# Attention of two layers rewritten: values as stationary column halves, probabilities weighed before their transpose

## The chip, the cores and the metric

The program runs on one core of one Trainium2 chip. The metric is device microseconds (us) of one execution; lower is better. The engines in the text are PE (matrix products and transposes), ACT (ScalarE), DVE (VectorE), POOL (GpSimd) and SP, which issues most DMAs.

## The reference

A two-layer transformer block for 256 tokens of width 1024, and one more attention layer behind it, all in float32. The layers, by the names that the kernel gives them:

- AB: `u = rms_norm(h)`; one wide projection `u @ w_in`; mixer A, 8 heads of 64: keys and values out of a latent of 256 (`w_uk`, `w_uv`), each query sees only the 64 keys that an index score ranks highest; mixer B, 8 heads of 64: causal softmax with a forget bias `cum[q] - cum[k]`; `h + concat(o_a, o_b) @ w_out`.
- MLP: `h + square(relu(rms_norm(h) @ w1)) @ w2`, hidden width 4096.
- C: 16 heads of 64 in two groups that share keys and values. Each head has three branches, each a softmax of its own, summed under sigmoid gates: `out = g0*o_c + g1*o_s + g2*o_w`, where o_c attends to 15 compressed blocks, o_s to selected blocks and o_w to a window. At 256 tokens o_s and o_w are two causal softmaxes over different keys and values. Then `h + o @ w_out`.
- MLP again, then the final norm.
- D: differential attention, 16 heads with two maps each, and its output projection.

For each query block of 128 tokens: `p = exp(s - m) / sum`, `o = p @ v`.

## The kernel before

The residual `h` stays in SBUF as two tiles of 128 tokens. Each weight block is loaded (SP), rounded to a high part `wH` (ACT or DVE) and a remainder `wL` (DVE), and each product is the sum of three PE products (H*H, H*L, L*H) in fp32r. Below, a *product* is one such instruction of 512 columns.

A softmax **map** is one head (in C one head and branch) on 256 queries. Its causal part is 128 x 128 for the first query block and 128 x 256 for the second, so a tile `E` of 128 x 384 holds it, queries on the partitions. The steps, for A, B and C alike:

1. `scores` or, in C, the fp32r products of `two_maps`: PE writes the scores into PSUM banks. In A, B and D two heads of 64 rows each run beside each other in the two row halves of the PE array.
2. `softmax_num`: DVE adds the mask and takes the minimum (two instructions), ACT takes the exponential with its sum (two instructions, each with a read of the accumulator).
3. `pv_part`: PE transposes E (three blocks) into a bank, ACT copies it into a tile `PT` (two of them), PE multiplies the transposed map (stationary, 128 columns) with the values (moving, 64 columns) in three products. In C `two_maps` does both branches of one head.
4. `finish`, once for four heads of A or B, or two of C: reciprocal of the sums, gates in C, DVE scales the output (queries on the partitions), in C two additions, then PE transposes it (`o_strand`), and it is rounded to H and L as the operand of the output projection. In C the compressed branch is multiplied for a whole group at once into a slot `oc` (`cmp_att`) and added here.

The division is thus made on the output. 48 maps go this way: 8 of A, 8 of B, 32 of C. D has maps of its own and keeps them.

**What sets the order.** All instructions are issued by a planner, `_Weaver`, at build time. Each piece of work is a strand, a Python generator that yields operations; the planner emits the operation that can start earliest by its own costs (`_Engine.cost`, `T`), ties by priority, so each engine's instruction stream is fixed when the program is built. An operation that more than one engine could do is yielded as a list, and the planner takes the smallest sum of ready time, cost and a toll (`W.toll`: 1.8 us for DVE in AB and C, 0.3 in D, 1.5 for POOL, none for ACT). Buffers are tokens: 8 PSUM banks, 8 `E`, 2 `PT`, 4 score tokens `S`, 14 slots of 4 KB per partition.

**The order of AB**: projections for the index, the small parts and A's queries, then `uk`, `uv`; A's attention; B's projections; B's attention; output rows 0 to 7. `out_proj` walks 4 rows of the weight over four pieces of the output, then for each piece the last 4 rows (in C: 7 rows, then the last).

Of the kernel before, what the change touches and what calls it, by code (L numbers as in the profile page):

```python
# [18 lines left out]
P = 128  # L19
# [82 lines left out]
class _Engine:  # L102
# [13 lines left out]
    def cost(self, name, a, kw):  # L116
# [16 lines left out]
        if kw.get("op") == ALU.pow:  # L133
            return 1e-3 * (300 + 165 * n)
# [127 lines left out]
def tile_kernel(ctx: ExitStack, tc: tile.TileContext, I: dict, out: bass.AP):  # L262
# [6 lines left out]
    slots = ctx.enter_context(tc.tile_pool(name="slots", bufs=14))  # L269
# [4 lines left out]
    NE, NPT, NS = 8, 2, 4  # L274
    W = _Weaver(B=8, E=NE, PT=NPT, S=NS, slot=14, n2=6, raw=3, w=8, rope=2, dup=3)
# [12 lines left out]
    HALF = 0  # L288
    T1W = 0
# [35 lines left out]
    def T(calls, beside=1):  # L325
        late = calls if callable(calls) else lambda: calls
        cost = work = 0.0
        for c in late():
            if len(c) == 3:
                cost += 0.109  # L330
                work += 0.053
            else:
                work += _free(c[0]) * (4 if c[1].dtype == F32 else 1) * c[1].shape[0] / 128 * 0.4167e-3
                cost += 0.003 + (4 * max(_free(c[0]), 128) if c[1].dtype == F32 else max(_free(c[0]), 256 if c[1].dtype == F32R else 128)) * 0.4167e-3
# [8 lines left out]
        return _Op("T", cost / beside, emit, None, work)  # L343
# [336 lines left out]
    def scores2(bs, qs, ks, stop=True):  # L680
        two = [scores(b, q, k, stop) for b, q, k in zip(bs, qs, ks)]
        return T([x for both in zip(*two) for x in both], 2)
# [12 lines left out]
    class Group:  # L695
# [7 lines left out]
        def start(self):  # L703
            if self.sums is None:
                self.sums = small(8, "sums", 6)

# [29 lines left out]

    def maps_strand(grp, qs, ks, evs, masks_of, vs, i, prio, bias=None):
        for e in evs:
            yield ("ev", e)
        yield ("acq", "E", 2)  # L740
        Es = [e384("E", NE) for _ in range(2)]
        masks = yield from masks_of(Es)
        yield ("acq", "S", 2)
        yield ("acq", "B", 2)
        bs = [bank(), bank()]
        yield scores2(bs, qs, ks, bias is None)
        if bias:
            yield T(bias(bs))
        grp.start()

        def free(te):
            W.give("B", te)
            W.give("S", te)

        def one(n):
            E = Es[n]
            yield from softmax_num(E, bs[n][:, 0:P], bs[n][:, P:3 * P], masks[n], grp.sums, 2 * (i + n), free)
            yield from pv_part(grp, E, vs[n], ((i + n) * P, (i + n) * P + 64), ((i + n) * P + 64, (i + n + 1) * P))

        W.spawn(one(1), prio + 1, W.end + 0.2)  # L760
        yield from one(0)
# [144 lines left out]
    def plan_ab():  # L906
        wv = kview(I["ab_w_in"][0])
        return dict(
            aqi=chunk(wv, [(784, 1296)], kpt=1), small=chunk(wv, [(512, 784), (1296, 1368), (2904, 2912)]),
            aq=chunk(wv, [(0, 512)]),  # L910
            uk=chunk(I["a_w_uk"][0].rearrange("(k p) h e -> p k (h e)", p=P), [(0, 384)], 2),
            uv=chunk(I["a_w_uv"][0].rearrange("(k p) h e -> p k (h e)", p=P), [(0, 512)], 2),
            bq=chunk(wv, [(1368, 1880)]), bk=chunk(wv, [(1880, 2392)]), bv=chunk(wv, [(2392, 2904)]),
            out=rows(kview(I["ab_w_out"][0]), range(8)))
# [12 lines left out]
    def layer_ab(pl, hin, hout):  # L927
# [144 lines left out]
        yield ("acq", "slot")  # L1072
        qA, qAev = kslot(slot()), pair()
        yield from proj(pl["aq"], heads_T(qA, qAev, -0.125), uop, uev)

        def ck(k, t):
            return ckH[:, k, t * P:(t + 1) * P], ckL[:, k, t * P:(t + 1) * P]

        yield ("acq", "slot", 2)
        kA, kAev = kslot(slot()), pair()  # L1080
        vA, vAev = slot().rearrange("p (t n) -> p t n", t=2), pair()
# [21 lines left out]

        yield from proj(pl["uk"], ev_k, ck, ckev)
        yield from proj(pl["uv"], ev_v(vA, rck, rckev, vAev), ck, ckev)
# [34 lines left out]
        def attention(qT, kT, v, evs, masks_of, bias, side, prio):  # L1140
            for g in range(2):
                def finish(grp, g=g):
                    rs = small(8, "rs", 4)
                    yield dve.reciprocal(out=rs, in_=grp.sums)
                    yield ("acq", "n2")
                    on = n2()
                    te = yield dve.tensor_tensor(
                        out=on.rearrange("p (t h d) -> p h t d", t=2, h=4),
                        in0=grp.ob.rearrange("p (h t d) -> p h t d", h=4, t=2),
                        in1=rs.rearrange("p (h t) -> p h t", h=4).unsqueeze(3).to_broadcast([P, 4, 2, 64]),  # L1150
                        op=ALU.mult)
                    W.give("B", te)
                    yield from o_strand(lambda j, t: on[:, t * S + j * P:t * S + (j + 1) * P],
                                        oH[side][:, 2 * g:2 * g + 2, :], oL[side][:, 2 * g:2 * g + 2, :],
                                        oev[4 * side + 2 * g:4 * side + 2 * g + 2])

                grp = Group(4, finish)
                for j in (0, 2):
                    hd = 4 * g + j
                    hi = [slice(0, 64), slice(64, 128)]  # L1160
                    vv = [[v[:, t, (hd + n) * 64:(hd + n + 1) * 64] for t in range(2)] for n in range(2)]
                    W.spawn(maps_strand(grp, [qT[x, hd // 2, :] for x in hi], [kT[x, hd // 2, :] for x in hi], evs,
                                        lambda Es, hd=hd: masks_of(hd, Es), vv, j, prio + hd,
                                        None if bias is None else (lambda bs, hd=hd: bias(bs, hd))), prio + hd)

        def masks_a(hd, Es):
            return [maskA, maskA]
            yield

        attention(qA, kA, vA, qAev + kAev + vAev + [maskev], masks_a, None, 0, 10)  # L1170
# [9 lines left out]
        def masks_b(hd, Es):  # L1180
            for n in range(2):
# [5 lines left out]
        def bias_b(bs, hd):  # L1187
            return [mm(bs[n][:, 0:3 * P], sel[:, hd + n, :], cumk, False, True) for n in range(2)]

        attention(qB, kB, vB, qBev + kBev + vBev + [cumev], masks_b, bias_b, 1, 20)  # L1190

        def opnd(k, t):
            return oH[k // 4][:, k % 4, t * P:(t + 1) * P], oL[k // 4][:, k % 4, t * P:(t + 1) * P]

        yield from out_proj(pl["out"], opnd, lambda k: oev[k], residual(hout))
# [8 lines left out]
    def layer_c(pl, hin, hout):  # L1204
# [185 lines left out]
        def cmp_att(g, Q, qev, oc, ocev):  # L1390
# [23 lines left out]
            summed = W.end  # L1414
            rc = small(16, "crc", 2)
            rcev = _Event()

            def sums():
# [4 lines left out]
                te = yield dve.tensor_tensor(out=rc.rearrange("p (t h) -> p t h", t=2),  # L1423
                                             in0=sc.rearrange("p (t h) -> p t h", t=2),
                                             in1=gates[:, :, 8 * g:8 * g + 8, 0], op=ALU.mult)
                rcev.set(te)

            W.spawn(sums(), 8 + 20 * g, summed)
            yield ("acq", "B")
            b = bank()  # L1430
            te = yield T([tr(b[:, t * P:(t + 1) * P], ec[:, t * P:(t + 1) * P]) for t in range(2)])
            yield ("acq", "n2")
# [422 lines left out]
```

## Time and profile before

| | |
|---|---|
| median of three runs | 924.11 us (922.16 to 925.39) |
| profiled execution | 921.53 us, span 919.4 us |
| PE busy in the span | 901.2 us, 98% |
| DVE, ACT, POOL busy | 64%, 56%, 12% |
| mean granted PE clock | 0.998 of full speed |

Start and end of the layers can be seen in PE's operands: AB ends with the first product of the MLP at 143.5 us, C reaches from about 325 to 464 us, D from 646 us to the end. A duration in the trace is that of one instruction from start to end; instructions of one engine overlap by some tenths of a us, so what one costs its engine is the distance from its start to the start of the next, called its pitch below. A timeline row with xN joins N like instructions.

### The profile page before, as it was taken

To read this page: it belongs to the slowest core of one execution; us is meant where nothing else is said; L and a number is where in the kernel's file an instruction comes from. 1 tells how busy PE (TensorE), PEld (TensorE's weight loads), DVE (VectorE), ACT (ScalarE), POOL (GpSimd) and SP (SyncE) were. 2 spreads that over 40 slices of the span, in tenths; PEclk is the share of its full clock that TensorE was granted. 3 is DMA by queue.
4 is the path that set the end of the run, shared out by engine and by line. 5 is a ranking of instruction groups with operands and counts; after the bars stand their busy time and mean duration, and the time that the engine had idled before them with its cause. 6 is when DMAs were issued, how large, how long until landed. Compare 5 with 4: busy or idle time off the path is not lost.

```text
span 919.4 us, 14126 instructions
## 1 busy us (share of the span) xinstructions
PE 901.2 (98%) x5196; PEld 766.9 (83%) x5196; DVE 586.6 (64%) x1230; ACT 518.2 (56%) x1025; POOL 106.4 (12%) x149
## 2 busy tenths in 40 slices
PE   8999999999999999999999999999999999999998
PEld 6778888999999878888789999998877778777786
DVE  5688646544454457766654445444878878697781
ACT  5666858455544564787575544455637545274450
POOL 3520000000000051120000000000310503204000
PEclk9999999999999999999999999999999999999999
DMA  7756134655555474312236665655674545544431
GB/s 233 207 178 211 55 104 164 203 183 187 189 191 190 133 249 143 110 46 70 74 123 196 208 192 179 198 184 161 161 220 130 159 138 160 165 133 159 140 115 46
DMA packets 65124, 144.55 MB, mean 157 GB/s; under 512 B 7214, under 2 KB 9744, under 8 KB 65056
## 3 DMA queue, kind: packets, MB, share of 16 engines
q1 hardware_dynamic: 63632, 140.68, 48.0%
q0 software_dynamic: 1424, 2.98, 1.6%
q8 instruction: 41, 0.67, 0.3%
q14 instruction: 27, 0.22, 0.1%
HBM read 142.59 MB, written 1.05 MB: 156 GB/s over the span
## 4 chain that ended last, share of the span: by engine, by line
PE 86%; DVE 4%; POOL 4%; DMA 3%; ACT 1%; issue 1%; SPq 0%; POOLq 0%; DVEq 0%; ACTq 0%
PE bank L341 81%; PE bank L339 5%; POOL qrs L113 2%; DVE wL L113 2%; DVE n L113 1%; DMA h<-in_x_dram 1%; ACT wH L113 1%; DMA raw<-in_c_w_in_dram 1%; POOL T L113 1%; POOL drn L113 1%; DMA raw<-in_ab_w_in_dram 1%; DVE qss L113 0%; DMA raw<-in_l_w_in_dram 0%; ACT n L113 0%; DVE dss L113 0%
## 5 line engine op out<-in xcount | busy, mean ns | idle before, releaser
L113 DVE TENSOR_TENSOR wL<-raw,wH 128x1024 fp32r<-128x1024 f32 (+2 forms) x262 | 317.8, 1214 | 187.9 <-ACT wH L113 186.2
L113 ACT CAST wH<-raw 128x1024 fp32r<-128x1024 f32 (+2 forms) x226 | 234.8, 1041 | 225.4 <-PE bank L341 181.4
L341 PE MATMUL bank<-wH,slot 128*128 128x512 f32 (+1 forms) x784 | 258.3, 396 | 1.2 <-ACT slot L113 0.6
L341 PE MATMUL bank<-wH,uH 128*128 128x512 f32 (+2 forms) x448 | 182.8, 408 | 0.5 <-ACT uH L113 0.5
L341 PE MATMUL bank<-wH,uL 128*128 128x512 f32 (+2 forms) x448 | 174.9, 390 | 0.0
L341 PE MATMUL bank<-wL,uH 128*128 128x512 f32 (+2 forms) x448 | 174.6, 390 | 0.0
L341 PEld LDWEIGHTS bank<-wH,slot 128*128 128x128 f32 x784 | 147.2, 188 | 32.1 <-issue 1.7
L341 PE MATMUL bank<-wL,slot 128*128 128x512 f32 (+1 forms) x392 | 152.7, 390 | 0.0
L341 PE MATMUL bank<-uH,wL 128*128 128x256 f32 x448 | 127.4, 284 | 0.0
L341 PE MATMUL bank<-uL,wH 128*128 128x256 f32 x448 | 127.0, 284 | 0.0
L341 PE MATMUL bank<-uH,wH 128*128 128x256 f32 x448 | 126.1, 281 | 0.0
L341 PEld LDWEIGHTS bank<-wH,uH 128*128 128x128 f32 x448 | 85.1, 190 | 20.2 <-issue 2.3
L341 PEld LDWEIGHTS bank<-wH,uL 128*128 128x128 f32 x448 | 84.8, 189 | 18.7 <-DVE uL L113 0.4
L341 PEld LDWEIGHTS bank<-wL,uH 128*128 128x128 f32 x448 | 85.2, 190 | 15.0 <-DVE wL L113 0.2
L341 PEld LDWEIGHTS bank<-uH,wH 128*128 128x128 f32 x448 | 85.0, 190 | 0.6
L341 PEld LDWEIGHTS bank<-uL,wH 128*128 128x128 f32 x448 | 84.3, 188 | 0.6
L341 PEld LDWEIGHTS bank<-wL,slot 128*128 128x128 f32 x392 | 73.8, 188 | 13.0
L341 PEld LDWEIGHTS bank<-uH,wL 128*128 128x128 f32 x448 | 84.6, 189 | 0.0
L113 ACT ACTIVATE E<-E,nb 128x128 f32<-128x128 f32 (+1 forms) x160 | 70.8, 447 | 9.7 <-DVE nb L113 9.6
L113 POOL TENSOR_TENSOR qrs<-qss,neghalf 128x8 f32<-128x8 f32 x16 | 36.3, 2272 | 141.6 <-DVE dss L113 110.0
L341 PEld LDWEIGHTS bank<-slot,PT 128*128 128x128 f32 x384 | 48.7, 191 | 3.9 <-issue 0.7
L113 POOL TENSOR_TENSOR r<-ms,neghalf 128x1 f32<-128x1 f32 x6 | 4.0, 668 | 403.3 <-DVE ms L113 403.3
(206 smaller groups left out, 953.4 us busy)
## 6 DMA issues: line engine op xcount, KB each, us to landing
raw<-in_mlp_w_dram SPq DMA_DIRECT2D x128, 512.0 KB, 3.9
raw<-in_l_w_in_dram SPq DMA_DIRECT2D x64, 512.0 KB, 3.8
raw<-in_ab_w_in_dram SPq DMA_DIRECT2D x16, 512.0 KB, 4.1
raw<-in_l_w_out_dram SPq DMA_DIRECT2D x16, 512.0 KB, 3.4
raw<-in_c_w_in_dram SPq DMA_DIRECT2D x12, 512.0 KB, 4.0
raw<-in_ab_w_out_dram SPq DMA_DIRECT2D x8, 512.0 KB, 3.4
raw<-in_c_w_out_dram SPq DMA_DIRECT2D x8, 512.0 KB, 3.5
slot<-in_ab_w_in_dram SPq DMA_DIRECT2D x8, 256.0 KB, 6.2
```

The source lines that it names most:

```text
L113: return _Op(self.key, self.cost(name, a, kw), lambda: f(*a, **kw), bank[0] if bank else None)
L339: i = pe.transpose(c[0], c[1], ident[:c[2], :c[2]])
L341: i = pe.matmul(c[0], lhsT=c[1], rhs=c[2], start=c[3], stop=c[4], skip_group_check=True)
```

## The change

The title line of the change says: A and B in strands of four heads, C in head pairs with all branches, values stationary by column halves, weighed maps transposed in place, B's attention first. In detail:

- A strand does four maps: four heads of A or B, or in C two heads with both branches. It holds four `E` from before the scores until its value products.
- Each map is divided by its sum (in C also multiplied with its gate) before the transpose: `weigh` scales the two query blocks of `E`, each by a column of 128 numbers. DVE, POOL and ACT are offered.
- `across` transposes E and copies the result back into E; `PT` is left to D.
- `pv_maps` makes the values stationary (64 columns) and the transposed map moving (256 and 128 columns). Two maps write the two halves of the partitions of one bank, which are column halves of the PE array, and both branches of C add up there; the compressed branch adds a product of 128 x 128 stationary and 256 moving columns for each head pair, out of weighed probabilities. The output comes out with its channels on the partitions.
- `o_round` rounds that to H and L: no scaling, no additions and no transposes of the output are left.
- B's projections and attention come before `aq`, `uk`, `uv` and A's attention; output rows 4 to 7 come first.
- Pools: 13 slots for 14, 10 `E` for 8. Planner: PE costs by instruction kind and a cost of 0.4 us for an operation in halves of the array, and a longer cost of the power on POOL.

```diff
         if kw.get("op") == ALU.pow:
-            return 1e-3 * (300 + 165 * n)
+            return 1e-3 * (380 + (175 if n < 8 else 262) * n)
...
-    slots = ctx.enter_context(tc.tile_pool(name="slots", bufs=14))
+    slots = ctx.enter_context(tc.tile_pool(name="slots", bufs=13))
...
-    NE, NPT, NS = 8, 2, 4
+    NE, NPT, NS = 10, 2, 4
...
+            mode = mode or c[1].shape[0] == 64 or _free(c[1]) == 64
+            if c[1].dtype == F32:
+                cost += 2 * max(0.112, 0.004 + 2 * n * 0.4167e-3)
+            elif c[1].dtype == F32R:
+                cost += max(0.112, 0.0145 + n * 0.4167e-3)
...
+        cost = cost / beside + (SWITCH if mode else 0.0)
...
+    def weigh(E, w):
+        for j, (a, z) in enumerate(HALVES):
+            yield [f.tensor_scalar(out=E[:, a:z], in0=E[:, a:z], scalar1=w[:, j:j + 1], scalar2=None, op0=ALU.mult)
+                   for f in (dve, pool)] + [act.activation(out=E[:, a:z], in_=E[:, a:z], func=AF.Copy, scale=w[:, j:j + 1])]
+
+    def across(E, there):
+        yield ("acq", "B")
+        b = bank()
+        yield T([tr(b[:, j * P:(j + 1) * P], E[:, j * P:(j + 1) * P]) for j in range(3)])
+        te = yield [act.copy(E, b[:, :384]), dve.tensor_copy(E, b[:, :384])]
+        W.give("B", te)
+        there.set(te + 0.2)
+
+    def pv_maps(grp, Es, vs, cols, there, more=None):
+        yield ("ev", there)
...
+            for i, col in enumerate(cols):
+                o = grp.ob[:, col:col + S]
+                out += [mm(o[hi[n], :], vs[2 * i + n][0], Es[2 * i + n][:, 0:S], first and i == 0, False) for n in range(2)]
+                out += [mm(o[hi[n], P:S], vs[2 * i + n][1], Es[2 * i + n][:, S:S + P], False, last) for n in range(2)]
...
+    def o_round(grp, H, L, evs):
+        bv = grp.ob.rearrange("p (j q) -> p j q", j=2)
+        yield [act.copy(H, bv), dve.tensor_copy(H, bv)]
+        te = yield dve.tensor_tensor(out=L, in0=bv, in1=H.bitcast(F32), op=ALU.subtract)
...
+        def one(n):
+            E = Es[n]
+            sums = small(2, "sums2", 12)
+            yield from softmax_num(E, bs[n][:, 0:P], bs[n][:, P:3 * P], masks[n], sums, 0, free)
+            yield dve.reciprocal(out=sums, in_=sums)
+            yield from weigh(E, sums)
+            yield from across(E, there)
...
-            out=rows(kview(I["ab_w_out"][0]), range(8)))
+            out=rows(kview(I["ab_w_out"][0]), (4, 5, 6, 7, 0, 1, 2, 3)))
```

**Where instructions stand now.** First ACT in the second half of C's attention. `E,sums` is the exponential with its sum, `PT` or `E<-bank` the copy of a transposed map, `wH` the rounding of a weight. Before, from the exponential of one map on:

```order
L113 ACTIVATE E_4479,sums_4436<-E_4479,nb_4480 128x128
L113 ACTIVATE E_4479,sums_4436<-E_4479,nb_4480 128x256
L113 ACTIVATE E_4489,sums_4436<-E_4489,nb_4490 128x128
L113 ACTIVATE E_4489,sums_4436<-E_4489,nb_4490 128x256
L113 COPY PT_4509<-bank_4504 128x384
L113 COPY PT_4516<-bank_4510 128x384
L113 CAST wH_4536<-raw_4375 128x1024
L113 ACTIVATE n2_4486<-n2_4486 128x256
```

Between its exponentials and the copy of its transpose, ACT does nothing to a map. After, ten rows from near the end of C's attention:

```order
L113 ACTIVATE E_4704,sums2_4723<-E_4704,nb_4724 128x128
L113 ACTIVATE E_4704,sums2_4723<-E_4704,nb_4724 128x256
L113 COPY E_4613<-bank_4774 128x384
L113 ACTIVATE E_4702<-E_4702,sums2_4712 128x256
L113 ACTIVATE E_4704<-E_4704,sums2_4723 128x128
L113 ACTIVATE E_4703,sums2_4746<-E_4703,nb_4747 128x128
L113 ACTIVATE E_4703,sums2_4746<-E_4703,nb_4747 128x256
L113 ACTIVATE E_4704<-E_4704,sums2_4723 128x256
L113 ACTIVATE E_4705,sums2_4758<-E_4705,nb_4759 128x128
L113 ACTIVATE E_4705,sums2_4758<-E_4705,nb_4759 128x256
```

The rows `E<-E,sums2`, two for each map, are new: all 96 scalings of the 48 maps stand on ACT and none on DVE or POOL, though all three are offered.

Second, PE at the end of AB's attention. `const,E` is the transpose of a map, `slot` with `wH` or `wL` a product of the output projection. Before, from the transposes of the last map on (`PT` is the transposed map in its value products):

```order
L339 MATMUL bank_1511<-const_81,E_1295 128x128 x3
L341 MATMUL bank_1261<-wH_984,slot_766 128x512
L341 MATMUL bank_1261<-wL_985,slot_766 128x512
L341 MATMUL bank_1261<-wH_984,slot_768 128x512
L341 MATMUL bank_1258<-wH_1003,slot_766 128x512
L341 MATMUL bank_1258<-wL_1004,slot_766 128x512
L341 MATMUL bank_1258<-wH_1003,slot_768 128x512
L341 MATMUL bank_1472<-slot_777,PT_1515 128x64 x3
L341 MATMUL bank_1259<-wH_1003,slot_766 128x512
```

Six products of the projection stand between the transposes of this map and its value products, and more follow behind. After, from the transposes of the last strand's second map on:

```order
L349 MATMUL bank_1525<-const_81,E_1440 128x128 x3
L349 MATMUL bank_1533<-const_81,E_1441 128x128 x3
L349 MATMUL bank_1551<-const_81,E_1442 128x128 x3
L351 MATMUL bank_1560<-E_1439,slot_1158 64x256
L351 MATMUL bank_1560<-E_1440,slot_1158 64x256
L351 MATMUL bank_1560<-E_1439,slot_1158 64x128
L351 MATMUL bank_1560<-E_1440,slot_1158 64x128
L351 MATMUL bank_1560<-E_1441,slot_1158 64x256
L351 MATMUL bank_1560<-E_1442,slot_1158 64x256
L351 MATMUL bank_1560<-E_1441,slot_1158 64x128
L351 MATMUL bank_1560<-E_1442,slot_1158 64x128
L351 MATMUL bank_1266<-wH_1331,slot_447 128x512
```

Now the last nine transposes, eight value products and the next product of the output projection (its operand `slot_447` is what `o_round` writes) stand directly behind each other. 42 products of the projection are left behind this point.

Elsewhere: in D the two transposes of the scaled keys, which follow the POOL power `qrs`, stood behind 18 and 30 products of the next projection and now stand behind 27 and 36; of the four score pairs of a group of D, two stood together and two alone, and in the first three groups they now stand two and two. In ACT's stream from the first exponential to the last rounding of the output (`slot<-bank` 128 x 512) there now stand, in AB: 16 pairs of exponentials, 32 scalings, 16 map copies, 8 casts of weights, 4 casts of the output, 10 evacuations of A's projections; in C: 32 pairs, 64 scalings, 32 copies, 8 casts of weights, 4 casts of the output, 4 evacuations of 64 x 512, and 6 smaller ones.

## Rows read from the trace of the kernel before

**Rows 1.** The page: engines, granted clock by slices, end of the chain by line.

```profile
PE 901.2 (98%) x5196; PEld 766.9 (83%) x5196; DVE 586.6 (64%) x1230; ACT 518.2 (56%) x1025; POOL 106.4 (12%) x149
...
PEclk9999999999999999999999999999999999999999
...
PE bank L341 81%; PE bank L339 5%; POOL qrs L113 2%; DVE wL L113 2%; DVE n L113 1%; DMA h<-in_x_dram 1%; ACT wH L113 1%; DMA raw<-in_c_w_in_dram 1%; POOL T L113 1%; POOL drn L113 1%; DMA raw<-in_ab_w_in_dram 1%; DVE qss L113 0%; DMA raw<-in_l_w_in_dram 0%; ACT n L113 0%; DVE dss L113 0%
```

**Rows 2.** The view by stretches; columns as its first line says, x counts instructions.

```profile
core 0: us, PE busy (x) PEld busy (x) DVE busy (x) ACT busy (x) POOL busy (x), PEclk, DMA share, GB/s
90.70:124.60 33.90, 33.90 (x251) 28.87 (x250) 20.43 (x90) 27.21 (x88) 0.00 (x0) 1.00 0.20 63
...
380.30:406.70 26.40, 26.36 (x197) 23.86 (x197) 20.18 (x93) 24.35 (x87) 2.93 (x6) 1.00 0.13 41
380.30:453.10 72.80, 71.67 (x489) 63.00 (x489) 51.21 (x203) 57.54 (x185) 7.81 (x14) 1.00 0.18 59
453.10:464.40 11.30, 8.80 (x49) 6.19 (x47) 6.95 (x15) 5.06 (x15) 0.00 (x0) 1.00 0.27 94
```

**Rows 3.** Timeline of PE in the AB attention: start, us, what, count.

```profile
88.64 1.58 PE L341 MATMUL bank<-slot 64*128 64x128 f32 x16
90.15 0.50 PE L341 MATMUL bank<-wH,uH 128*128 128x512 f32 x1
...
102.19 1.45 PE L341 MATMUL bank<-slot,PT 128*128 128x64 f32 x12
103.47 0.83 PE L339 MATMUL bank<-const,E 128*128 128x128 f32 x6
104.05 0.48 PE L341 MATMUL bank<-wH,slot 128*128 128x512 f32 x1
...
106.21 0.93 PE L341 MATMUL bank<-slot 64*128 64x128 f32 x8
107.07 0.62 PE L341 MATMUL bank<-cumk,slot 72*128 72x384 f32 x2
107.52 0.40 PE L341 MATMUL bank<-wH,slot 128*128 128x512 f32 x1
107.76 0.40 PE L341 MATMUL bank<-wL,slot 128*128 128x512 f32 x1
```

**Rows 4.** Timeline of ACT in the C attention, same columns.

```profile
384.73 0.39 ACT L113 ACTIVATE E<-E,nb 128x128 f32<-128x128 f32 x1
385.02 0.19 ACT L113 ACTIVATION_READ_ACCUMULATOR E<-E,nb 128x1 f32 x1
385.11 0.50 ACT L113 ACTIVATE E<-E,nb 128x256 f32<-128x256 f32 x1
385.51 0.19 ACT L113 ACTIVATION_READ_ACCUMULATOR E<-E,nb 128x1 f32 x1
385.94 0.42 ACT L113 ACTIVATE n<-n 128x256 f32<-128x256 f32 x1 [0.24 <-DVE n L113]
386.26 0.39 ACT L113 ACTIVATE E<-E,nb 128x128 f32<-128x128 f32 x1
...
387.14 0.83 ACT L113 COPY PT<-bank 128x384 f32<-128x384 f32 x2
387.87 0.38 ACT L113 COPY n<-bank 128x256 f32<-128x256 f32 x1
```

**Rows 5.** Timeline of ACT after the AB layer: scaling by a column.

```profile
143.09 1.13 ACT L113 ACTIVATE n<-bank,gcol 128x128 f32<-128x128 f32 x4
144.09 1.06 ACT L113 CAST wH<-raw 128x1024 fp32r<-128x1024 f32 x1
145.03 0.64 ACT L113 CAST uH<-n 128x512 fp32r<-128x512 f32 x1
```

**Rows 6.** Timeline of ACT: first exponential and last map copy of AB, of C.

```profile
90.72 0.40 ACT L113 ACTIVATE E<-E,nb 128x128 f32<-128x128 f32 x1 [1.62 <-DVE nb L113]
...
124.12 0.48 ACT L113 COPY PT<-bank 128x384 f32<-128x384 f32 x1 [0.91 <-PE bank L339]
...
380.33 0.40 ACT L113 ACTIVATE E<-E,nb 128x128 f32<-128x128 f32 x1 [2.48 <-DVE nb L113]
...
452.25 0.86 ACT L113 COPY PT<-bank 128x384 f32<-128x384 f32 x2
```

**Rows 7.** Timeline of PE: first product of the layer after AB, end of C.

```profile
143.49 0.39 PE L341 MATMUL bank<-wH,uH 128*128 128x512 f32 x1
...
457.39 0.50 PE L341 MATMUL bank<-wH,slot 128*128 128x512 f32 x1 [0.64 <-ACT slot L113]
...
458.71 0.73 PE L341 MATMUL bank<-wH,slot 128*128 128x512 f32 x2 [0.59 <-DVE slot L113]
...
464.43 0.50 PE L341 MATMUL bank<-wH,uH 128*128 128x512 f32 x1 [0.51 <-ACT uH L113]
```

**Rows 8.** Groups of ACT instructions in 380.3 to 453.1 us, by form: busy us, mean ns, idle.

```profile
L113 ACT COPY PT<-bank 128x384 f32<-128x384 f32 x32 | 14.3, 479 | 5.3 <-PE bank L339 5.1
...
L113 ACT CAST wH<-raw 128x1024 fp32r<-128x1024 f32 x8 | 8.4, 1046 | 1.0 <-PE bank L341 0.8
L113 ACT CAST slot<-bank 128x256 fp32r<-128x256 f32 x7 | 2.6, 369 | 1.9 <-PE bank L339 1.8
L113 ACT ACTIVATE slot<-bank 64x512 fp32r<-64x512 f32 x4 | 2.4, 590 | 1.8 <-PE bank L339 1.7
```

**Rows 9.** Timeline of PE in the D layer, at the transposes of k.

```profile
729.29 0.40 PE L341 MATMUL bank<-wH,uL 128*128 128x512 f32 x1
730.40 0.66 PE L339 MATMUL bank<-const,n 128*128 128x128 f32 x4 [0.71 <-DVE n L113]
...
734.03 0.41 PE L339 MATMUL bank<-const,n 128*128 128x128 f32 x2 [0.21 <-DVE n L113]
```

**Rows 10.** Timeline of POOL at the same place.

```profile
727.08 2.48 POOL L113 TENSOR_TENSOR qrs<-qss,neghalf 128x8 f32<-128x8 f32 x1 [4.58 <-DVE qss L113]
```

**Rows 11.** Groups of PE instructions in 646 to 919.4 us, by form: the transposes of n.

```profile
L339 PE MATMUL bank<-const,n 128*128 128x128 f32 x96 | 14.2, 276 | 3.0 <-DVE n L113 3.0
```

More of the change, by code (lines that the diff above doesn't have):

```diff
@@ L288, in tile_kernel @@
     HALF = 0
+    SWITCH = 0.4
     T1W = 0
@@ L342, in emit @@
             return i
-        return _Op("T", cost / beside, emit, None, work)
+        return _Op("T", cost, emit, None, work)
     def events(n, m):
@@ L680, in scores2 @@
     def scores2(bs, qs, ks, stop=True):
-        two = [scores(b, q, k, stop) for b, q, k in zip(bs, qs, ks)]
-        return T([x for both in zip(*two) for x in both], 2)
+        maps = [scores(b, q, k, stop) for b, q, k in zip(bs, qs, ks)]
+        return T([x for n in range(0, len(maps), 2) for both in zip(*maps[n:n + 2]) for x in both], 2)
     HALVES = ((0, P), (P, 3 * P))
@@ L735, in pv_part @@
             W.spawn(grp.finish(grp), FIN, te + 0.2)
[L737 to L761, printed above, removed]
     def o_strand(nat, H, L, evs, gp=None, width=2):
@@ L1142, in finish @@
                 def finish(grp, g=g):
[L1143 to L1170, printed above, removed]
+                    yield from o_round(grp, oH[side][:, 2 * g:2 * g + 2, :], oL[side][:, 2 * g:2 * g + 2, :],
+                                       oev[4 * side + 2 * g:4 * side + 2 * g + 2])
+                grp = Group(1, finish)
+                hi = [slice(64 * (n % 2), 64 * (n % 2) + 64) for n in range(4)]
+                hd = [4 * g + n for n in range(4)]
@@ L1180, in masks_b @@
         def masks_b(hd, Es):
-            for n in range(2):
+            for n in range(4):
                 yield [_run(*(f.tensor_scalar(out=Es[n][:, a:z], in0=causal[:, a:z], scalar1=cumq[:, t, hd + n:hd + n + 1],
@@ new lines, in maps_of, with finish_of @@
+                W.spawn(head(1), prio + 2, W.now)
+                v2 = [[vsw[:, t, y, 64 * g:64 * g + 64] for t in range(2)] for y in range(2)]
+                more = (pcev, vBD[g][:, 2 * hp:2 * hp + 2, :].rearrange("p h d -> p (h d)"), lambda: pc[0], used)
+                W.spawn(pv_maps(grp, Es[0] + Es[1], [v2[0], v2[0], v2[1], v2[1]], ((hp % 2) * S,) * 2, there, more), prio)
+                yield from head(0)
+            def finish_of(gp):
+                def finish(grp):
+                    ks = slice(2 * gp, 2 * gp + 2)
+                    yield from o_round(grp, oH[g][:, ks, :], oL[g][:, ks, :], oev[4 * g + 2 * gp:4 * g + 2 * gp + 2])
+                return finish
@@ L1555, in layer_c @@
+            for gp in range(2):
+                grp = Group(2, finish_of(gp))
+                for hp in (2 * gp, 2 * gp + 1):
+                    prio = 10 + 20 * g + 4 * hp
+                    W.spawn(maps_of(grp, hp, prio), prio)
         for g in range(2):
```

216 lines of the change are left out of this document (119 added, 97 removed).

## The prediction

> **What bounds the kernel now.** I read the page first. PE is busy for 901 of 919 us, its clock is granted in full in every slice, and the chain that ends last runs over PE [rows 1]. So the kernel is bound by PE almost everywhere, and what PE saves should come out of the time, as long as no other engine has as much to do in the stage concerned. That is why the view by stretches came next, cut at the first exponential and the last map copy of each attention on ACT [rows 6]: 90.7 to 124.6 us in AB, 380.3 to 453.1 us in C. In C's 72.8 us PE is busy for 71.7, ACT for 57.5 and DVE for 51.2; in AB's 33.9 us PE all the time, ACT for 27.2 [rows 2]. PE is the limit there, but ACT has only 15 us to spare in C and 7 in AB. Those two numbers decide this case. The MLP layers, about 363 us, keep their instructions and I leave them at zero.
>
> **What PE saves.** The value products of two maps are 12 records (each float32 product is two): from 102.19 to 103.47, 1.28 us [rows 3]. All 48 maps make 24 pairs, 30.7 us. For the new form, halves of the array, the nearest row is the scores: heads beside each other in the row halves, with the same 128 and 256 moving columns. Two heads take 106.21 to 107.07, 0.86 us; four in one go take 88.64 to 90.15, 1.51 us, so each change into and out of the halves costs about 0.2 [rows 3]. The new value products go four maps at a time: 12 x 1.51 = 18.1 us. If column halves didn't run beside each other, two maps would cost 1.28 us as before, since twice the columns move: 31 us. I take 18.1, 12.6 us less. Four maps to an operation also spare A and B three or four changes in the scores, 0.7 us. The 32 transposes of outputs go, at (104.05 - 103.47)/6 = 0.10 us each: 3.2 us. The compressed branch stays as large (half the columns, twice the instructions): 0. PE has 16.5 us less to do, about 10 in C and 6.5 in AB.
>
> The Trainium skill (TensorEngine Tiling (Array Packing), "Stationary-Streaming Swap + Column Tiling" under Performance Considerations) names just this swap for a moving side of 64 columns, with up to twofold speed. No run here shows column halves yet; by that the value products would come to 15.4 us, 2.7 less than the rows of the scores make them.
>
> **What ACT gets.** The order shows all 96 scalings on ACT. What one costs isn't in the trace in this form, so I bound it. By the pitch of the exponentials, which also read a column as bias: 385.02 - 384.73 = 0.29 and 385.51 - 385.11 = 0.40, together 0.69 us a map [rows 4]. From below: four scalings by a column take 144.09 - 143.09 = 1.00 us, 0.25 each for 128 columns [rows 5], and a pass over 256 columns without a column operand 386.26 - 385.94 = 0.32 [rows 4]: 0.57 us. I take 0.66, nearer to the exponentials, which have the same operands. The rest of a map: exponentials with their reads (385.51 - 384.73 + 0.10 =) 0.89 us, copy (387.87 - 387.14)/2 = 0.37, with the single ones 0.39 [rows 4, 8]. A map is then 0.89 + 0.66 + 0.39 = 1.94 us of ACT (1.83 to 1.98).
>
> C, counted from the order: 32 maps 62.1 us; 8 weight casts at 0.97 and 4 evacuations at 0.60 (the means of [rows 8], the casts less the overlap with the next instruction), 10.2; 4 output casts at 0.55 (an estimate between the 0.37 for 256 columns [rows 8] and the 0.64 for 512 [rows 5]), six small ones at 0.43 (by the 0.32 and 0.37 of [rows 4], two being twice as wide), 4.8. Sum 77.1 us (73.6 to 78.4) from the first exponential to the last rounding, in a stage that took 72.8. ACT does not run without gaps: in its densest stretch before, 380.3 to 406.7, it is busy for 24.35 of 26.40 us [rows 2]. With that share of gaps, 8%, the stage takes 83.3 us: **+10.5 us**. PE's 62 us lie beside it and no longer show. What is queued on ACT behind a scaling that waits for its reciprocal, gate or sum are the next map's exponentials, the copies for PE and the weight casts, so PE waits there too. Behind the last copy, before, 11.3 us pass till the next layer's first product [rows 2, 7], a good 2 of them in waits for the rounding of the output. Now both last rows of the projection wait for it, 24 products behind the last value products: about +1. The first scores come 3 products (0.7 us) earlier. C: +10.8.
>
> AB, the same way: 16 maps 31.0 us, 8 weight casts 7.8, 4 output casts 2.2, 10 evacuations of A's projections at 0.60 as above 6.0: 47.0 us, with gaps 50.8. It starts earlier, since 24 products of `uk` and `uv` (4.9 us) and 16 transposes (1.6) now come behind the first scores, while four heads and the bias take 0.9 us more than two pairs without it: first exponential at 90.7 - 5.6 = 85.1. ACT is through at 135.9. Then the remainder on DVE and two hand-offs (457.39 to 458.71 for the like, 1.3 us [rows 7]), 42 products at 0.23 [rows 3] and 12 transposes, 11.0: the next layer starts at 148.2, before at 143.5 [rows 7]. **+4.7 us**. By PE alone it would start near 137.
>
> DVE could have taken the scalings: it is idle for 21 us of C's 72.8 [rows 2]. Its toll of 1.8 us in the planner keeps it out.
>
> The Trainium skill warns of this (TensorEngine Tiling (Array Packing), "PSUM Bottleneck"): tiling speeds up TensorE but not the evacuation of PSUM, and both ScalarE and VectorE are to be used for it. Here rows 2 agree as to how little ACT has to spare.
>
> **What D gains.** After each projection of keys PE waits for POOL's power, 2.48 us, and DVE's scaling behind it [rows 9, 10]: between 729.29 and 730.40 passes 1.11 us where a product takes 0.23 [rows 3]; before the second transposes it waits 0.21. Over D the waits for `n` are 3.0 us [rows 11]. The new order puts 9 and 6 products (2.1 and 1.4 us) more in front of them: gone. Per group that is 0.88 and about 0.3 us, over D some 3.4. Two score pairs that now stand together spare a change of 0.2 in three groups. Closer together now: the transposes of a map and its value products, three products between for six; I take half a us off for that. **-3.5 us** (-5 to -1). 13 slots for 14 let the third group's output tiles come later; only the projection at the end needs them: 0. SP issues the same loads, B's ahead of A's; POOL loses six additions; the top-k of the index on DVE now has B's projections and attention over it instead of holding up the first scores: 0, since PE didn't wait there.
>
> **Sum**: 921.5 + 10.8 + 4.7 - 3.5 = 933.5 us for the profiled execution. Its 921.5 lies 2.6 below the median of the three runs, so the median is forecast at **936 us**: slower.
>
> **Rivals.**
> - A: PE stays the limit. Then 16.5 us of PE and D's 3.5 come off: 901.5, median 904. For it speaks that PE bounds every stage now; against it that ACT would have to do at least 73 us of work in C in 62. Chance 4%.
> - B: ACT fills up without gaps, since two strands are always in flight and the order was laid out for it. C 77.1 (+4.6 with its end), AB 47.0 (next layer at 144.4, +0.9), D -3.5: +2.0, median 926; with the lowest price of a scaling C is 73.6 (+1.1) and AB 45.2 (-0.9), and with D at -5 the median is 919 at the least. For it: in C's first half before, ACT was busy for 92%. Against it: ACT waits for transposes and for sums on other engines in either half [rows 8]. This is the case on the other side, not slower; it decides where the gaps fall below 3%. Chance 17%.
> - C: the strands are too few. Ten `E` hold two strands of four maps, and a third can't start its scores until all four maps of the first have been scaled, transposed, copied and multiplied; at that hand-over ACT runs dry. With 20% gaps C takes 92 (+20), AB 56 (+10), D -3.5: 948, median 951. For it: before, an `E` came free behind its transposes, now behind the value products. Against it: while one strand is in its last steps, the other has up to 8 us of ACT left. Chance 13%.
> - The forecast, gaps of 4 to 14%: 929 to 944, chance 66%.
>
> A difference below 0.3% (2.8 us) can't be told from none with this kernel. Faster: A and a third of B, 9%; same: the rest of B and a little of the forecast, 14%; slower 77%. The range that leaves out A, the lower third of B and the upper half of C is 920 to 950.
>
> **What would show it.** Right: in C, ACT busy for over 90% from the first exponential to the last copy, this stretch 80 to 87 us long; PE there at or below 80% busy, waiting for ACT's `E`; the MLP of the first layer starting near 148 us of the span; value products of two maps in 0.6 to 0.9 us; no wait of PE for `n` of over 0.5 us in D. Wrong: C's stretch below 75 us, or ACT idle for a fifth of it (then C), or value products of 1.3 us a pair, which on top of ACT's load would show as PE busy throughout.

## The result and the profile after

| | before | after |
|---|---|---|
| median | 923.13 us (921.05 to 925.39, 4 runs) | 937.31 us (936.57 to 938.67, 4 runs) |
| ratio | | 1.0149, 95% interval 1.0124 to 1.0173 |
| span of the profiled execution | 919.4 us | 935.9 us |
| PE busy | 901.2 us | 905.5 us |
| ACT busy | 518.2 us | 541.3 us |
| mean granted PE clock | 0.998 | 0.982 |

The change costs 1.5%; the forecast was 936 us. The total was met by errors that nearly cancel, as the stages of the two profiled executions show. The stages begin and end as in the prediction [rows 6, 7]; the times of after are its first exponentials and last map copies on ACT and the first product of each next layer on PE.

| stage | before | after | difference | forecast |
|---|---|---|---|---|
| start to AB's first exponential | 90.7 | 84.4 | -6.3 | -5.6 |
| AB, first exponential to last map copy | 33.9 | 50.9 | +17.0 | +16.9 |
| from there to the MLP's first product | 18.9 | 15.4 | -3.5 | -6.6 |
| MLP and C's front, to C's first exponential | 236.8 | 242.9 | +6.1 | -0.7 |
| C, first exponential to last map copy | 72.8 | 76.8 | +4.0 | +10.5 |
| from there to the MLP's first product | 11.3 | 11.6 | +0.3 | +1.0 |
| MLP | 181.6 | 182.0 | +0.4 | 0 |
| D | 273.4 | 271.9 | -1.5 | -3.5 |
| sum (span) | 919.4 | 935.9 | +16.5 | +12.0 |

The page of the changed kernel answers to [rows 1]; the last row is from its groups (busy, mean, then idle time before them and what ended it).

```profile
PE 905.5 (97%) x5076; PEld 754.5 (81%) x5076; DVE 585.0 (63%) x1265; ACT 541.3 (58%) x1106; POOL 103.9 (11%) x143
...
PEclk9999989999999997989999999999999999999999
...
PE bank L351 71%; ACT E L113 7%; PE bank L349 3%; ACT wH L113 2%; DVE wL L113 2%; ACT n L113 1%; POOL T L113 1%; ACT slot L113 1%; DMA raw<-in_l_w_in_dram 1%; DMA slot<-in_ab_w_in_dram 1%; DMA raw<-in_c_w_in_dram 1%; DVE E L113 0%; POOL r L113 0%; DMA raw<-in_ab_w_in_dram 0%; DMA raw<-in_mlp_w_dram 0%
...
L349 PE MATMUL bank<-const,E 128*128 128x128 f32 x192 | 35.1, 291 | 13.5 <-ACT E L113 12.2 <-DVE slot L113 1.1
```

Three things are new. The chain now runs over ACT's `E` for 7% of the span, where before no ACT row had over 1%. PE waits 12.2 us for ACT before the transposes of maps, that is, for scaled maps. And the clock row has two 8s and a 7 where it was 9 throughout (a 9 stands for 90% or more of a slice). The view by stretches tells where (columns as its first line says); it answers to [rows 2].

```profile
core 0: us, PE busy (x) PEld busy (x) DVE busy (x) ACT busy (x) POOL busy (x), PEclk, DMA share, GB/s
84.40:135.30 50.90, 44.05 (x273) 32.94 (x272) 21.68 (x91) 45.99 (x133) 2.91 (x8) 0.97 0.25 81
...
393.60:470.40 76.80, 67.60 (x412) 51.37 (x414) 46.52 (x225) 76.40 (x245) 3.03 (x8) 0.95 0.15 49
...
360.64:374.30 13.66, 13.66 (x58) 12.79 (x57) 5.03 (x22) 0.95 (x4) 0.00 (x0) 0.50 0.17 58
...
135.36:142.19 6.83, 6.16 (x19) 4.51 (x18) 2.16 (x3) 0.59 (x1) 0.00 (x0) 0.50 0.48 154
```

In C, ACT is busy for 76.40 of 76.80 us: it is the limit, and it has no gaps. In AB it is busy for 45.99 of 50.90. The last two rows are stretches in which PE's clock was granted at 0.50, its level of 1.2 GHz: 13.7 us ahead of C's attention, 6.8 us in AB's projection. What PE did there is in its timeline (start, us, what, count, idle before and its releaser):

```profile
132.66 0.33 PE L349 MATMUL bank<-const,E 128*128 128x128 f32 x1 [1.19 <-ACT E L113]
134.00 0.44 PE L349 MATMUL bank<-const,E 128*128 128x128 f32 x2 [1.01 <-ACT E L113]
134.36 2.47 PE L351 MATMUL bank<-E,slot 128*64 128x256 f32 x16
137.51 0.79 PE L351 MATMUL bank<-wH,slot 128*128 128x512 f32 x1 [0.68 <-ACT slot L113]
...
353.57 0.45 PE L349 MATMUL bank<-const,dup 128*128 128x128 f32 x2 [1.34 <-DVE peT L113]
...
356.68 1.87 PE L351 MATMUL bank<-n,slot 128*128 128x30 f32 x16
...
359.67 0.69 PE L349 MATMUL bank<-const,dup 128*128 128x128 f32 x2 [0.34 <-DVE dup L113]
360.19 3.04 PE L351 MATMUL bank<-n,slot 128*128 128x30 f32 x16
363.05 0.67 PE L349 MATMUL bank<-const,dup 128*128 128x128 f32 x2
...
364.79 6.87 PE L351 MATMUL bank<-n,slot 128*128 128x30 f32 x32
...
445.01 1.52 PE L351 MATMUL bank<-E,slot 128*64 128x256 f32 x16
446.46 0.88 PE L349 MATMUL bank<-const,E 128*128 128x128 f32 x6
```

`n,slot` with 30 columns are the products of C's compressed branch. 16 records take 1.87 us at 356.68; the 32 from 364.79, twice as many, take 6.87, 3.7 times as long. Before 135.36 PE had waited twice for ACT's maps, 1.19 and 1.01 us. The last pair of rows times the new value products: four maps are 16 records in 446.46 - 445.01 = 1.45 us.

ACT's timeline in C prices the scaling (`E<-E,sums`; starts tell the pitch); it answers to [rows 4].

```profile
425.24 0.41 ACT L113 ACTIVATE E<-E,sums 128x128 f32<-128x128 f32 x1
425.53 0.41 ACT L113 ACTIVATE E<-E,nb 128x128 f32<-128x128 f32 x1
...
428.14 0.54 ACT L113 ACTIVATE E<-E,sums 128x256 f32<-128x256 f32 x1
428.55 0.42 ACT L113 ACTIVATE E<-E,nb 128x128 f32<-128x128 f32 x1
```

0.29 + 0.41 = 0.70 us a map, the price of the exponentials. Last, D's transposes of `n`, the group of [rows 11], and the one wait over 0.5 us that is left:

```profile
L349 PE MATMUL bank<-const,n 128*128 128x128 f32 x96 | 14.6, 276 | 1.0 <-DVE n L113 0.9
```

```profile
695.49 0.66 PE L349 MATMUL bank<-const,n 128*128 128x128 f32 x4 [0.56 <-DVE n L113]
```

### The profile page after: what moved, and what is told of

It reads as the page before. It is cut to its first block, busy times and chain, and to the rows that moved or that the text cites. A ratio compares the mean times of both kernels' runs of the same rounds, so it can differ in the third digit from the quotient of the medians.

```text
span 935.9 us, 14027 instructions
## 1 busy us (share of the span) xinstructions
PE 905.5 (97%) x5076; PEld 754.5 (81%) x5076; DVE 585.0 (63%) x1265; ACT 541.3 (58%) x1106; POOL 103.9 (11%) x143
## 4 chain that ended last, share of the span: by engine, by line
PE 74%; ACT 11%; issue 5%; DVE 4%; DMA 3%; POOL 2%; SPq 0%; ACTq 0%; DVEq 0%; POOLq 0%
PE bank L351 71%; ACT E L113 7%; PE bank L349 3%; ACT wH L113 2%; DVE wL L113 2%; ACT n L113 1%; POOL T L113 1%; ACT slot L113 1%; DMA raw<-in_l_w_in_dram 1%; DMA slot<-in_ab_w_in_dram 1%; DMA raw<-in_c_w_in_dram 1%; DVE E L113 0%; POOL r L113 0%; DMA raw<-in_ab_w_in_dram 0%; DMA raw<-in_mlp_w_dram 0%
## 5 line engine op out<-in xcount | busy, mean ns | idle before, releaser
L113 DVE TENSOR_TENSOR wL<-raw,wH 128x1024 fp32r<-128x1024 f32 (+3 forms) x262 | 318.2, 1217 | 189.4 <-ACT wH L113 187.9
L113 ACT CAST wH<-raw 128x1024 fp32r<-128x1024 f32 (+2 forms) x218 | 226.6, 1042 | 220.6 <-PE bank L351 195.5
L351 PEld LDWEIGHTS bank<-wL,uH 128*128 128x128 f32 x448 | 85.1, 190 | 14.8
L349 PE MATMUL bank<-const,E 128*128 128x128 f32 x192 | 35.1, 291 | 13.5 <-ACT E L113 12.2
L349 PEld LDWEIGHTS bank<-const,E 128*128 128x128 f32 x192 | 23.3, 144 | 24.1 <-ACT E L113 17.5
```

Of the source, the lines that this page charges most:

```text
L113: return _Op(self.key, self.cost(name, a, kw), lambda: f(*a, **kw), bank[0] if bank else None)
```

## The experiments

Eleven kernels. Each was timed beside the kernel before on the same chip, and the ratio given is to that (923.13 above; 922.49 beside e1 to e4, 923.88 beside e5 to e8, 923.86 beside e9 to e11). The theory: ACT's work sets both attention stretches, and the planner's new PE costs, not the attention, lost time in C's front. The rival: the strands' hand-overs, or PE's work, set the stretches.

### e1_front: the order of before in C's front

```diff
         cost = cost / beside + (SWITCH if mode else 0.0)
+        if OLD[0]:   # True from C's first projection to the end of its first q projection
+            cost = sum(0.109 if len(c) == 3 else
+                       0.003 + (4 * max(_free(c[0]), 128) if c[1].dtype == F32 else max(_free(c[0]), 256)) * 0.4167e-3
+                       for c in late()) / beside
```

> The changed kernel with one difference: while the planner lays out the projections ahead of C's attention it costs PE's operations by the formula of before, so that PE gets the 30-column products of the compressed branch in the order of before (fours, with weight products between) in place of clumps of 8, 8 and 16; the attention keeps its order. Theory (the clumps let PE's granted clock fall to 0.50 from 360.6 to 374.3 us, and that is what C's front lost): the fall goes or shrinks to the 3.4 us of before, the stretch from C's start to its first exponential goes from 61.0 back to 55 to 57 us, the whole to 931 to 934. Rival (the front is late for its loads or for the slots, and the low clock only fills the wait): the stretch stays at 59 to 61 us and the time at 935 to 938.

Measured: 932.91 us, 1.0101 (1.0077 to 1.0126). Its view by stretches, C's front and C's attention:

```profile
332.90:385.00 52.10, 49.93 (x288) 42.07 (x286) 34.08 (x77) 27.49 (x52) 19.13 (x42) 1.00 0.60 196
385.00:462.60 77.60, 69.16 (x410) 53.05 (x410) 45.73 (x224) 75.79 (x244) 3.02 (x8) 0.91 0.16 48
```

(Both cuts here are the last transpose of the residual and C's first exponential; the same stretch was 53.4 us before and 59.3 after.) With the 30-column products in portions of 8 and 16 records between weight products the clock stays at full in this stretch, and it is 7.2 us shorter. ACT's stretch stays. So 4.4 us of the change's 14 (937.3 less 932.9) come from an order that its planner costs brought, and that nothing in C's arithmetic asks for. The theory holds for the order of the front as a whole; that the portions are what counts in it is argued, since the edit moves other work there too.

### e2_front_dve and e4_front_half: scalings off ACT

```diff
 e2: all on DVE
-                   for f in (dve, pool)] + [act.activation(...)]
+                   for f in (dve,)]
 e4: the 256 columns of the second block on DVE, the 128 of the first on ACT
-                   for f in (dve, pool)] + [act.activation(...)]
+                   for f in (dve, pool)][:1] if j else [act.activation(...)]
```

> e1 and all 96 scalings on DVE. Theory (ACT's work sets both attention stretches: 76.4 of 76.8 us busy in C, 46 of 50.9 in AB): ACT loses 0.71 us a map, 22.7 us in C and 11.4 in AB; DVE gets about 0.5 a map, 16 us and 8; then PE (about 62 in C at full clock), DVE (62) and ACT (54) are near each other, C's ACT stretch goes from 76.8 to 64 to 70 us, AB's from 50.9 to 40 to 45, the whole to 911 to 921. Rival 1 (the four-map strands and their hand-overs set the time, ACT is only where it shows): the stretches stay within 3 us and ACT gets idle instead, 928 to 934. Rival 2 (DVE becomes the limit at once, since its chain of mask, minimum, reciprocal, gate and scaling is one engine's): C 72 to 78, AB 46 to 50, 925 to 933.

> e1 with the wide scaling (256) of each map on DVE and the narrow one (128) left on ACT: ACT loses 0.41 us a map, 13.2 us of 76.1 in C and 6.7 of 45.2 in AB. Theory (ACT's work sets the stretch): C's ACT stretch 64 to 68 us, AB's 42 to 46, the whole 914 to 923, and by the same rule as e2 the time follows ACT's sum until PE's 62 stand. Rival (hand-overs): within 3 us of e1.

Measured: e2 914.03 us, 0.9907 (0.9875 to 0.9938); e4 913.77 us, 0.9897 (0.9874 to 0.9920), 0.2 below the range expected. First e2's stretches of AB and C, then e4's:

```profile
85.00:123.30 38.30, 38.30 (x258) 30.33 (x257) 29.65 (x122) 34.11 (x100) 3.09 (x8) 1.00 0.35 110
375.80:446.00 70.20, 63.95 (x395) 49.07 (x395) 57.49 (x287) 54.31 (x179) 3.89 (x8) 0.93 0.16 47
```

```profile
85.30:129.40 44.10, 42.04 (x271) 31.48 (x271) 26.94 (x107) 39.84 (x117) 3.00 (x8) 1.00 0.33 107
378.80:445.60 66.80, 63.59 (x410) 49.91 (x410) 53.12 (x257) 63.34 (x212) 3.15 (x8) 0.97 0.19 60
```

Against e1, 19 us go by moving 48 or 96 small instructions to an engine that had time, and the change is then faster than before. AB falls from 50.9 us to 38.3 in e2, where PE is busy throughout, and to 44.1 in e4. In C, e4 follows ACT's sum (63.34 of 66.80); e2 has no full engine any more and takes longer, with 10.2 us of the clock at 0.50. Both rivals fall.

### e3_before_costs and e7_costs_front: the planner's costs alone

```diff
 e3: the kernel before with the cost functions of the change (T, pow, SWITCH = 0.4)
 e7: e3 with OLD as in e1
```

> The kernel before with only the planner's new costs (PE by kind with 0.4 us for halves, POOL's longer power): no instruction is changed, only the order. Theory (D's gain and C's front come from the costs, not from the attention): D 1 to 3 us shorter than 273.4, no wait of PE for n over 0.75 us there, and a fall of the clock in C's front worth 1 to 4 us; the whole 921 to 926. Rival (D gains because of 13 slots and ten E): D stays at 273.4 and the whole within 0.3% of 923 unless the front falls.

> e3 (before with the planner's new costs) with the costs of before while C's projections and compressed branch are laid out, as in e1. Theory (e3's 7 us are the low clock in C's front: 17.1 us at 0.50 against 3.4 before): the whole comes back to 921 to 925, C's front to 53 to 55 us, and D keeps its shorter groups. Rival (the costs hurt before's attention, with 0.4 us put on each operation in halves): 926 to 930.

Measured: e3 929.46 us, 1.0063 (1.0043 to 1.0083), 3.5 above the range expected; e7 922.18 us, 0.9982 (0.9968 to 0.9996). e3 in its low stretch, then e7 in C's front:

```profile
357.76:371.42 13.66, 13.66 (x52) 12.31 (x52) 3.24 (x12) 1.55 (x3) 0.00 (x0) 0.50 0.12 38
```

```profile
329.30:380.50 51.20, 49.37 (x288) 42.20 (x286) 34.29 (x77) 27.71 (x53) 17.62 (x42) 1.00 0.64 198
```

The same 13.66 us at 0.50 in a kernel whose attention is that of before: the costs make it, and with the old order in that one place the 7 us are gone. It repeats: the mean granted clock is 0.988 to 0.991 in the four executions of e3 and 0.996 to 0.999 in the nine of e7. Groups of D follow each other at 55.5 us in both (696.8 to 753.2 is 56.4 before, 715.3 to 770.8 is 55.5 after, first exponentials), so D's gain is the costs' too, and needs neither 13 slots nor ten `E`.

### e5_halves_in_turn and e10_dve_in_turn: what PE's saving is worth

```diff
-            for i, col in enumerate(cols):
-                o = grp.ob[:, col:col + S]
-                out += [mm(o[hi[n], :], vs[2 * i + n][0], Es[2 * i + n][:, 0:S], first and i == 0, False) for n in range(2)]
-                out += [mm(o[hi[n], P:S], vs[2 * i + n][1], Es[2 * i + n][:, S:S + P], False, last) for n in range(2)]
+            for n in range(2):
+                for i, col in enumerate(cols):
+                    o = grp.ob[:, col:col + S]
+                    out.append(mm(o[hi[n], :], vs[2 * i + n][0], Es[2 * i + n][:, 0:S], first and i == 0, False))
+                    out.append(mm(o[hi[n], P:S], vs[2 * i + n][1], Es[2 * i + n][:, S:S + P], False, last))
```

> e1 with the value products of four maps issued half by half: first every product into the lower half of the partitions, then every one into the upper half, so that neighbours write the same column half and can't run beside each other. If the two halves ran beside each other in the changed kernel (16 records in 1.45 us), they now take near 2.9 us: 12 times 1.4 is 17 us more for PE, 11 of them in C and 6 in AB. Theory (ACT's work sets both stretches, PE's saving lies beside it): C's ACT stretch 77 to 81 us, AB's 51 to 54, the whole 933 to 940. Rival (PE's work still counts): 944 to 950.

> e6 with the value products half by half, as in e5 (there 2.2 us in place of 1.5 for four maps, and 2.6 us of the whole). With the scalings off ACT, PE is busy for all of AB's stretch and 63.5 of 66.7 us in C, so the same 12 x 0.7 = 8 us of PE should now show. Theory (PE sets the stretches again): 912 to 917. Rival (ACT still sets C): only AB's third shows, 909 to 911.

Measured: e5 935.50 us, 1.0113 (1.0094 to 1.0132), 2.6 above e1 (1.1 by the two ratios); e10 916.00 us, 0.9917 (0.9885 to 0.9949), 7.7 above e6 below. PE's timeline in e5, one strand of four maps, against the 1.52 above:

```profile
428.20 2.22 PE L356 MATMUL bank<-E,slot 128*64 128x256 f32 x16
```

Half by half the four maps take 0.7 us more (not 1.4: the expected doubling was wrong). These 12 x 0.7 = 8 us show almost whole when ACT is not the limit, and for a third at most when it is. That is the clearest evidence that in the changed kernel PE's saving lay beside ACT's work.

### e6_dve_and_half: the better part of each

```diff
+            yield on_dve if all_dve or j else on_act     # all_dve: in A and B
```

> The better part of e2 and e4: all scalings of A and B on DVE, in C the wide ones on DVE and the narrow ones on ACT. By the layers of e2 and e4 (AB's last transposes of the residual for the next layer end at 140.1 us in e2 and 145.0 in e4; from there to the same point behind C 137.9 us in e2 and 130.1 in e4) the sum is about 5 us below e4: 907 to 911. Rival (the layers' times hang on where the clock falls, not on the engines' shares): anything from 909 to 918, with a fall of the granted clock in C that e4 did not have.

Measured: 908.27 us, 0.9826 (0.9807 to 0.9846): 1.7% below the kernel before, 29 us below the changed one. AB and C by stretches:

```profile
85.10:123.40 38.30, 38.30 (x258) 30.33 (x257) 29.65 (x122) 34.09 (x100) 3.08 (x8) 1.00 0.36 109
373.60:440.30 66.70, 63.54 (x409) 49.77 (x410) 53.10 (x256) 63.29 (x212) 3.15 (x8) 0.97 0.19 59
```

PE and ACT are now level in C. The layers add up as expected.

### e8_a_first and e11_dve_a_first: A's attention first

```diff
 the blocks of A (aq, uk, uv, attention) ahead of those of B; weights and output rows in that order
```

> e1 with A's projections and attention ahead of B's, as in the kernel before (weights and output rows in that order too); scalings on ACT. Theory (B first gives ACT its 47 us of work an earlier start, 85.5 us against about 91): the next layer starts 2 to 5 us later than in e1, the whole 934 to 938. Rival 1 (the order decides nothing, ACT's sum does): within 2 us of e1. Rival 2 (with A first, ACT's work lies beside the long projections of B, and the tail is B's alone): the next layer starts 4 to 8 us earlier, the whole 924 to 929.

> e6 with A ahead of B, as in e8. With PE as AB's limit the order should matter by what PE finds to do at the end: with A last, the 40 products of uk, uv and the projection's first rows lie beside A's maps; with B last, only the projection. Theory: the next layer starts 1 to 4 us later than in e6, the whole 909 to 913. Rival (order without effect, as e8 stood to e1): 907 to 910.

Measured: e8 931.82 us, 1.0083 (1.0063 to 1.0103), the same as e1, so that my theory fell and rival 1 stands; e11 916.60 us, 0.9927 (0.9902 to 0.9952), 8.3 above e6 and slower than either expectation. AB's attention in e11:

```profile
86.10:129.70 43.60, 42.62 (x272) 32.95 (x271) 34.58 (x138) 34.85 (x98) 0.00 (x0) 1.00 0.35 110
```

With ACT as the limit the order is worth nothing measurable in the whole (in the profiled executions the next layer does start 3.3 us later in e8, 152.6 against 149.3, but C's ACT stretch is 2.7 us shorter, and neither was followed up). With PE as the limit B first is worth 5.2 us: the next layer starts at 143.0 us in e11 and at 137.8 in e6. The rest of the 8 us lies elsewhere: e11's profiled execution, 3.0 us above its median, has 6.8 us at 0.50 in C's front, and C's attention takes 70.1 us where it took 66.7. Whether A first brings that, by the planner's timing, or something else does, is open.

### e9_toll_half: one number of the planner

```diff
-    TOLL1 = 1.8
-    TOLL2 = 1.8
+    TOLL1 = 0.5
+    TOLL2 = 0.5
```

> e1 with one number of the planner changed: the toll that it puts on DVE in AB, C and the MLPs is 0.5 us for 1.8. By its order 24 of the 96 scalings, 11 map copies (in D too) and more casts of weights go to DVE. Theory (ACT's sum sets both stretches): ACT loses about 20 us of work in all, C's ACT stretch 64 to 70 us, AB's 42 to 48, the whole 914 to 923. Rival (DVE's remainders of the weights come late behind these, PE waits for them in the MLPs): the MLPs grow by over 1 us each and the whole is 923 to 930.

Measured: 923.45 us, 0.9999 (0.9981 to 1.0017), just outside the theory's range and inside the rival's.

```profile
381.90:455.10 73.20, 65.75 (x413) 50.14 (x414) 52.79 (x247) 65.48 (x223) 5.39 (x8) 0.95 0.20 58
146.90:328.80 181.90, 181.90 (x1131) 164.02 (x1130) 97.82 (x101) 94.86 (x129) 2.90 (x4) 1.00 0.59 186
```

The first MLP is 0.7 us longer than in e1 (181.2), the second, from its first product to the last transposes of the residual, is no longer (182.9 against 183.2), so the rival's reason does not hold. ACT's work in C falls from 75.79 to 65.48 us, but the stretch only from 77.6 to 73.2: ACT's sum sets a lower bound, and here the stretch stays 8 us above it, with 6.8 us of the clock at 0.50. Why the gaps come back was not tested.

## Why the forecast came out

**Right, and shown: who becomes the limit.** ACT has 76.4 us of work in a stretch that took 72.8. The forecast counted 77.1; the scaling was put at 0.66 us and is 0.70, the upper bound, and the rest came out some 2 us lower (0.6 of it the last rounding, which falls behind this stretch). e2, e4 and e6 take it off and the time follows; e5 and e10 put work on PE and it shows only where ACT has been relieved. The Trainium skill's warning (TensorEngine Tiling (Array Packing), "PSUM Bottleneck") is that tiling speeds up TensorE but not the evacuation of PSUM, for which both ScalarE and VectorE are to be used. e4's 19 us point the same way, but what it shares is scalings of `E`, not the evacuation that the page speaks of; no run here moved that alone.

**Right: PE's saving.** Value products of four maps took 1.45 us against 1.51 forecast from the scores: 12 x 1.45 = 17.4 us. The row of the scores was a good guide, and e5 shows that most of the gain hangs on neighbours in the stream writing different halves: four maps took 2 x 1.28 = 2.56 us before, 2.15 half by half (from start to the next start, 428.20 to 430.35) and 1.45 alternating. By the twofold speed that the Trainium skill (TensorEngine Tiling (Array Packing), "Stationary-Streaming Swap + Column Tiling") names, an estimate for all 48 maps is 15.4 us, 2.0 below the 17.4 measured.

**Right in time: AB's stretch**, 84.4 to 135.3 us against 85.1 to 135.9, though its gaps have another cause than the one they were taken from (below).

**Wrong: the gaps of ACT in C.** The term "with that share of gaps, 8%" added 6.2 us; ACT had 0.4 us of gaps. I took the share from a stretch in which PE was the limit, so ACT's gaps there were its waits for PE. In C, where ACT is the limit with two strands in flight, its queue did not run dry: rival B's mechanism was true there, though not for AB (10% gaps). There most of the gap is one wait, between the maps of A's two strands (ACT's timeline of after, and PE's ahead of it):

```profile
122.08 0.73 PE L351 MATMUL bank<-wH,slot 128*128 128x512 f32 x2 [1.03 <-DVE slot L113]
...
123.20 1.58 PE L351 MATMUL bank<-slot 64*128 64x128 f32 x16
...
124.50 0.40 ACT L113 ACTIVATE E<-E,nb 128x128 f32<-128x128 f32 x1 [3.74 <-DVE nb L113]
```

The last strand's scores, at 123.20, stand behind the value products of eight maps and six products of the output projection, one of which waits 1.03 us for DVE's rounding. That is the hand-over of rival C, at one place, worth 3.7 us; no run tested it with more `E`. The evidence named for C's length (80 to 87 us) and PE's share (at most 80%; it was 88%, partly at 0.50) failed by the missing gaps.

**Wrong: C's front and AB's end at no cost.** I read the order for the places of the attention and of D, and took the rest as unmoved. The new costs had also moved the 30-column products of the compressed branch together, and the granted clock fell to 1.2 GHz for 13.7 us: the stage lost 6.1 us where I had put -0.7. At AB's end, PE's waits for ACT ahead of the last value products were followed by 6.8 us at 0.50 (half of it, 3.4 us, lost; 3.1 are missing from the forecast of that stage). This fall is not the order's alone: e1 has the same instructions in AB and the same two waits of 1.19 and 1.01 us, and in its profiled execution the clock stayed at 1.00 there and the stage took 13.0 us, 0.7 above the forecast. In neither place did the trace of before show a low clock, but C's front had the warning at 345.47 us, 3.4 us at 0.50 behind a wait of 1.8. The prediction read the page's row of 9s as a full clock, and in a slice of 23 us such a stretch still leaves a 9.

**Mis-sized: D.** The waits for `n` fell from 3.0 to 1.0 us: I had counted all of them, with some 0.4 us around them, as gone, but the first group kept its 0.29 and got a new wait of 0.56, against the sign that none over 0.5 would be left. D gained 1.5, not 3.5.

**The sum.** -6.5 in C, +6.8 ahead of it, +3.1 at AB's end, +2.0 in D, -0.9 in the small rest: 12.0 became 16.5 between the two profiled executions. Between the medians it is 14.2, since before's profiled execution lay 1.6 us under the median of its four runs and after's 0.4 above. That 936 met 937.3 was luck: the gaps that were forecast in C did not come, and a low clock that nobody forecast took their place. Without the 6.8 and 3.1 us an estimate from these stages is 937.3 - 9.9 = 927.4 us, near the 926 of rival B.

## What to carry to other kernels

When a change relieves the bounding engine, add up what it gives to each other engine in that stage before anything else: here 0.7 us for each of 48 maps on ACT, with part of one stage at the lower clock, made a loss of 14 us out of what is a gain of 15.6 in e6, where two thirds of the scalings go to DVE and C's front keeps its old order. Take the share of gaps from a stretch in which that engine is the limit, not from one where it waits for another. When a planner's costs change, read the whole order again, above all where short products stand in small portions between long ones.

## What the runs showed of the hardware

- The granted clock fell to 0.50 at 360.64 us of the changed kernel although PE had been idle for only 0.34 us since 356.68 (its last longer wait, 1.34 us, ended at 353.57): what it did from there on were 30-column products, with three weight products and a pair of transposes between. The same 64 records in portions of 8 and 16 in place of 16 and 32, with more weight products between, kept 1.00 in e1 and e7. At 0.50, 32 of them took 6.87 us against 2 x 1.87.
- The same instructions do not always get the same clock: AB's end ran its first 6.8 us at 0.50 in after and at 1.00 in e1, behind the same waits.
- For products into two column halves the order counts: 16 records lasted 1.52 us with the halves alternating, 2.22 us half by half.
- The scaling of 128 x 256 by a column lasts 528 ns on ACT and 341 ns on DVE (groups of after and of e2), 128 x 128 lasts 419 and 286.
